# Moving feature tile 0 of a normed input to another byte distance from the weight tiles, in a two-layer decoder trunk

## The chip, the cores and the metric

One core of a Trainium2 chip runs the whole program in one launch. The metric is the device time of one execution in microseconds (us). TensorE (PE, with its weight loads as PEld) multiplies, VectorE (DVE) and ScalarE (ACT) split operands and do the elementwise work, SyncE (SP) issues nearly all weight transfers.

## The reference, cut to what matters

Two layers on 256 tokens of width 1024; everything is float32.

```python
x = x + short_conv_mixer(rms_norm(x, a_norm), a_w_in, a_conv, a_w_out)      # mixer A
x = x + conv_glu_ffn(rms_norm(x, f_norm[0]), f_w_up[0], f_conv[0], ...)     # first feed-forward
k, v = shared_kv(rms_norm(x, kv_norm), w_k, w_v)
x = x + moba_attention(rms_norm(x, b_norm), b_w_q, b_w_o, k, v, ...)        # mixer B
x = x + conv_glu_ffn(rms_norm(x, f_norm[1]), f_w_up[1], f_conv[1], ...)     # second feed-forward
return rms_norm(x, final_norm)

def conv_glu_ffn(h, w_up, conv_w, conv_b, w_down):
    u = causal_dwconv(h @ w_up, conv_w) + conv_b
    g, v = split(u, 2)                        # d_ff = 2816 each
    return (silu(g) * v) @ w_down
```

## The kernel before, in words

**Products.** The float32 product of a weight tile and an input tile is taken as three products of fp32r parts: high weight by high input, high weight by low input, low weight by high input. `mm3` (L164 to L166) issues these three matmuls. In each, the 128x128 weight part is the stationary operand, loaded by PEld, and a 128x256 input part (128 features, 256 tokens) is the moving one. The normed input is held as `xh` and `xl`, eight feature tiles (k = 0 to 7) of 256 columns, 1024 bytes per partition each. The norm's gain is in them; its row factor is applied to the result, so a unit can start before the norm's sum is known.

**Units.** A weight unit is one column block: "B" units of 128x2048 (two output tiles, `m` = 2) and "S" units of 128x1024. SP loads `raw`, ACT writes the high part `hi` (L86), DVE the low part `lo` (L92). `up_step` runs the 48 matmuls of a B unit (8 feature tiles, 2 output tiles, 3 products) or the 24 of an S unit into one PSUM bank. A feed-forward has 22 up units, and 22 down units that follow with a lag of three. In the first feed-forward the down products are `mm3` too (24 matmuls of 256 columns, gated hidden parts `sh`, `sl` moving). In the second they are `token_bank` (L189 to L191): 12 matmuls of 512 columns, with the hidden parts stationary and the weights moving. The V projection (L555 to L558) also has its weights moving and its input parts stationary.

**Order.** The order of each engine is that of the code (a manual schedule). PE runs through the stream of units almost without a pause. What stands between units, and is called a break below, is `rstd_cols` (L305: 128x1 matmuls of the sum of squares), `rstd_rows` (L319: a matmul that spreads the row factor), `bias_table` (L330), and in mixer B the transposes, scores and probability products. `rstd_cols` and `rstd_rows` come once in each of mixer A (within units MC[1] and MC[2]), the first feed-forward (unit 1 and behind it), the V projection and the second feed-forward (unit 1 and behind it). `bias_table` stands in mixer A ahead of unit MC[4].

**Addresses.** `shifted` (L242) makes the tiles of `xh` and `xl`: 64 floats longer than needed, with the data from float 48, that is 192 bytes in. The hidden parts `sh` and `sl` begin at float 16 of tiles that the pool places 128 bytes further, modulo 256, than the weight tiles. Every `hi` and `lo` tile and both buffers of `xh` and `xl` are placed at one remainder modulo 256 bytes, and every step within them is a multiple of 256 bytes. So whenever an input part moves against a weight part, the moving operand starts 192 bytes behind the stationary one, modulo 256. This is called the distance below. Where a weight moves against an input part (the V projection, the second feed-forward's down products) it is 64.

Of the kernel before, what the change touches and what calls it, by code (L numbers as in the profile page):

```python
# [12 lines left out]
F32R = mybir.dt.float32r  # L13
I32 = mybir.dt.int32
AF = mybir.ActivationFunctionType
OP = mybir.AluOpType

S = 256
D = 1024
KT = D // 128  # L20
# [12 lines left out]
P_AN, P_KVN, P_BN, P_FN, P_FIN, P_CONV, P_FCW, P_FCB = 0, 8, 16, 24, 40, 48, 72, 336  # L33
# [4 lines left out]
def f32(ap):  # L38
    return ap.bitcast(F32)
# [3 lines left out]
def yoco_kernel(ctx: ExitStack, tc: tile.TileContext, t: dict, out: bass.AP):  # L43
    nc = tc.nc
    V, A, G, PE = nc.vector, nc.scalar, nc.gpsimd, nc.tensor
# [3 lines left out]
    act = ctx.enter_context(tc.tile_pool(name="act", bufs=2))  # L49
# [12 lines left out]
    class Unit:  # L62


        def __init__(self, src, n, slots=(0, 1, 2)):
            self.src, self.n, self.tag = src, n, "B" if n == BIG else "S"
            self.raw = self.hi = self.lo = None
            self.used = False
            mine = by_tag[self.tag]
            self.at = len(mine)  # L70
            last = {s: max([u.at for u in mine if u.slot == s], default=-1) for s in slots}
            self.slot = min(slots, key=lambda s: (last[s], s))
            self.prev = mine[last[self.slot]] if last[self.slot] >= 0 else None
            mine.append(self)
# [22 lines left out]
    def hi(tag, part=0, parts=1):  # L97

        n = ptr[tag][0]
        if n < len(by_tag[tag]) and (by_tag[tag][n].prev is None or by_tag[tag][n].prev.used):  # L100
            by_tag[tag][n].split_hi(part, parts)
            ptr[tag][0] += part == parts - 1
# [11 lines left out]
    MC = [Unit(t["w_mc"][j], BIG) for j in range(KT)]  # L114
# [48 lines left out]
    def mm3(o, wh, wl, xh, xl, start, stop):  # L163
        PE.matmul(o, wh, xh, start=start, stop=False, skip_group_check=True)  # L164
        PE.matmul(o, wh, xl, start=False, stop=False, skip_group_check=True)  # L165
        PE.matmul(o, wl, xh, start=False, stop=stop, skip_group_check=True)  # L166

    def up_step(u, o, xh, xl, m, ks=range(KT)):

        assert u.lo is not None  # L170
        wh, wl = u.v(u.hi, m), u.v(u.lo, m)
        for k in ks:
            for i in range(m):
                mm3(o[:, i, :], wh[:, k, i, :], wl[:, k, i, :], xh[:, k, :], xl[:, k, :],
                    start=(k == 0 and i == 0), stop=(k == KT - 1))
        u.used = ks[-1] == KT - 1

    def down_bank(u, b, acc, hh, hl, first, last):
# [61 lines left out]
    def shifted(pool, name, tag, rows, **kw):  # L240

        t = pool.tile([128, rows * S + 64], F32R, name=name, tag=tag, **kw)  # L242
        return t[:, 48:48 + rows * S].rearrange("p (k s) -> p k s", s=S)

    def parts_tiles():
        return shifted(act, "xh", "xh", KT), shifted(act, "xl", "xl", KT)

    def scaled_hi(x, gain, ks, xh, order=same):
        for k in ks:
# [10 lines left out]
    def sum_squares(sq, half, order=same):  # L260

        f = 4 * half
        V.tensor_add(sq[:, f:f + 2, :], sq[:, f:f + 2, :], sq[:, f + 2:f + 4, :])
        if half:
            V.tensor_add(sq[:, 0:2, :], sq[:, 0:2, :], sq[:, 4:6, :])
            V.tensor_add(sq[:, 2, :], order(sq[:, 0, :]), order(sq[:, 1, :]))
# [1 line left out]
    def square_tile():  # L268
        return act.tile([128, KT, S], F32, name="sq", tag="oh", bufs=1)

    def boundary(acc, x, gain, order=same):

        xh, xl = parts_tiles()
        sq = square_tile()
        for q in range(5):
            if q < 4:
                V.tensor_add(x[:, 2 * q:2 * q + 2, :], acc[q], x[:, 2 * q:2 * q + 2, :])
                scaled_hi(x, gain, (2 * q, 2 * q + 1), xh, order)
            if q:
                scaled_lo(x, gain, (2 * q - 2, 2 * q - 1), xh, xl, order)  # L280
                squares(x, sq, q - 1)
        sum_squares(sq, 0)
        for part in range(2):
            lo("B", part, 2)
        sum_squares(sq, 1, order)
        return xh, xl, sq
# [77 lines left out]
    for q in range(4):  # L364
# [3 lines left out]
        if q == 2:  # L368
            sum_squares(sq, 0)
    sum_squares(sq, 1)  # L370
    hi("S")
    lo("S")
    rr = None
# [24 lines left out]
        zl()  # L398

    mc[1] = acc_bank()  # L400
    up_step(MC[1], mc[1], xh, xl, 2, range(0, 6))
    _, dg = rstd_cols(sq)
    for q in range(4):
        hi("B", q, 4)
        lo("B", q, 4)
    hi("S")
    hi("B")
    up_step(MC[1], mc[1], xh, xl, 2, range(6, 8))
    mb[1] = acc_bank()
    up_step(MB[1], mb[1], xh, xl, 1)  # L410
    mc[2] = up_bank()
    up_step(MC[2], mc[2], xh, xl, 2, range(0, 2))
    rr = rstd_rows(dg)
    A.activation(rr[:, 1, :], rr[:, 0, :], AF.Square)
    lo("S")
    up_step(MC[2], mc[2], xh, xl, 2, range(2, 8))
    mb[2] = psum.tile([128, 512], F32, name="misc", bufs=1).rearrange("p (a s) -> p a s", s=S)
    up_step(MB[2], mb[2], xh, xl, 1)
    for i in range(2):
# [17 lines left out]
    bias_table()  # L437
    for j in range(4, KT):
        mc[j] = up_bank()
        up_step(MC[j], mc[j], xh, xl, 2)  # L440
        o = mixer_a(j, "S")
        mb[j] = up_bank()
        up_step(MB[j], mb[j], xh, xl, 1)
        hi("S")
        mixer_b(j, o, "B" if j < KT - 1 else "S")
        if j < KT - 1:
            lo("S")
        if j == KT - 3:
            lo("B")
        down_step(MO[j - 2], acc, z[j - 2])  # L450
        hi("S")
        if j == KT - 1:
            lo("S")
    down_last(MO[KT - 2:], acc, [z[KT - 2], z[KT - 1]])
    xh, xl, sq = boundary(acc, xT, P_FN)
    hi("S")


# [2 lines left out]
    def ffn(layer, xh, xl, sq, bank=down_bank, between=None):  # L461
        ub, hd, low = {}, {}, {}
        up, dn = UP[layer], DN[layer]

        def conv(j, last=False):
            c0 = 2 * FJ * layer + j
            cw = [[par(P_FCW, 3 * (c0 + half * FJ) + n) for n in range(3)] for half in range(2)]
            u = tmp.tile([128, 2, S], F32, name="u", bufs=2)
            V.tensor_mul(u, ub[j], rr[:, 0:1, :].to_broadcast([128, 2, S]))  # L469
            if j:  # L470
                low[j - 1]()
            if not last:
                lo("B")
            o = tmp.tile([128, 2, S], F32, name="cv", bufs=2)
            for half in range(2):
                A.activation(o[:, half, :], u[:, half, :], AF.Identity, scale=cw[half][2],  # L476
                             bias=par(P_FCB, c0 + half * FJ))
            hi("B")
            for back in (1, 2):
                for half in range(2):  # L480
                    tap(o[:, half, :], u[:, half, :], cw[half][2 - back], back)
            return o

        def gate(j, o, last=False):
            sl = tmp.tile([128, S], F32, name="sl", tag="sc", bufs=3)
            hi("S")
            A.activation(sl, o[:, 0, :], AF.Silu)
            lo("S", 0, 1 + last)
            hid = tmp.tile([128, S], F32, name="hid", tag="pr", bufs=4)
            V.tensor_mul(hid, sl, o[:, 1, :])  # L490
            hd[j], zh, low[j] = split_act(hid, S)
            zh()
            if last:
                lo("S", 1, 2)
                low[j]()

        acc = None
        for i in range(FJ):
            ub[i] = up_bank()
            if i == 1:  # L500
                up_step(up[1], ub[1], xh, xl, 2, range(0, 3))
                _, dg = rstd_cols(sq)
                lo("S")
                A.activation(first, ones[:, 0:1], AF.Silu)
                up_step(up[1], ub[1], xh, xl, 2, range(3, 8))
                rr = rstd_rows(dg)
                gate(0, conv(0))
            else:
                up_step(up[i], ub[i], xh, xl, 2)
            last = i == FJ - 1  # L510
            if i:
                o = conv(i, last)
                if not last:
                    gate(i, o)
            if i == 0 and between:
                between()
            if i >= LAG:
                if i == LAG:
                    acc = [acc_bank() for _ in range(4)]
                down_step(dn[i - LAG], acc, hd[i - LAG], first=(i == LAG), bank=bank)  # L520
            if last:
                gate(i, o, True)
            elif i == FJ - 2:
                hi("S")
                lo("S")
            if i == 0:
                hi("B")
        if bank is token_bank:
            token_last(dn[FJ - 3:], acc, [hd[j] for j in range(FJ - 3, FJ)])
        else:  # L530
            down_step(dn[FJ - 3], acc, hd[FJ - 3])
            down_last(dn[FJ - 2:], acc, [hd[FJ - 2], hd[FJ - 1]])
        return acc
# [223 lines left out]
    wo(4)  # L757
    wo(5)
    down_last(WO[KT - 2:], acc, [(oh[:, j, :], ol[:, j, :]) for j in (KT - 2, KT - 1)])
    xh, xl, sq = boundary(acc, xT, P_FN + KT)  # L760
    hi("B")
    lo("B")
    hi("S")
# [128 lines left out]
```

## Time and profile before

| | |
|---|---|
| runs of the kernel | 590.6, 594.22, 589.56 us (median 590.6) |
| the profiled execution | 590.07 us |
| its span | 588.2 us |
| outside the span | 1.87 us |
| mean granted TensorE clock over the span | 0.996 |
| PE busy | 579.7 us, 99% of the span, 4745 matmuls |
| PEld busy | 564.4 us, 96% |
| DVE busy, ACT busy | 460.6 us (78%), 359.0 us (61%) |

The span is from the first instruction to the end of the last; PE's busy time counts matmuls that overlap in a pipeline, so that the pace of the stream is read from the starts of the matmuls and not from the busy share.

### The profile page before, as it was taken

To read this page: it belongs to the slowest core of one execution; us is meant where nothing else is said; L and a number is where in the kernel's file an instruction comes from. 1 tells how busy PE (TensorE), PEld (TensorE's weight loads), DVE (VectorE), ACT (ScalarE), POOL (GpSimd) and SP (SyncE) were. 2 spreads that over 40 slices of the span, in tenths; PEclk is the share of its full clock that TensorE was granted. 3 is DMA by queue.
4 is the path that set the end of the run, shared out by engine and by line. 5 is a ranking of instruction groups with operands and counts; after the bars stand their busy time and mean duration, and the time that the engine had idled before them with its cause. 6 is when DMAs were issued, how large, how long until landed. Compare 5 with 4: busy or idle time off the path is not lost.

```text
span 588.2 us, 11533 instructions
## 1 busy us (share of the span) xinstructions
PE 579.7 (99%) x4745; PEld 564.4 (96%) x4745; DVE 460.6 (78%) x779; ACT 359.0 (61%) x568; POOL 3.7 (1%) x15
## 2 busy tenths in 40 slices
PE   9999999999999999999999999999999999999995
PEld 8999999999999999999999999999999999999994
DVE  5898769888887778877987997668997778777865
ACT  7665337566665556555758998648675455545443
POOL 0000000000000000000000000000000000000001
PEclk9999999999999999999999999999999999999998
DMA  8985583447545654555456564424555654553111
GB/s 292 402 283 188 167 299 109 155 144 266 183 167 198 216 215 178 168 194 180 144 170 236 184 217 162 152 100 150 209 198 196 216 191 160 188 214 119 61 37 72
DMA packets 24236, 108.51 MB, mean 184 GB/s; under 512 B 2759, under 2 KB 5496, under 8 KB 16248
## 3 DMA queue, kind: packets, MB, share of 16 engines
q1 hardware_dynamic: 23864, 107.46, 51.5%
q8 instruction: 37, 0.61, 0.4%
q10 hardware_dynamic: 320, 0.32, 0.2%
q14 instruction: 15, 0.12, 0.1%
HBM read 106.70 MB, written 1.07 MB: 183 GB/s over the span
## 4 chain that ended last, share of the span: by engine, by line
PE 96%; DMA 1%; ACT 1%; SPq 0%; DVE 0%; issue 0%; POOLq 0%; POOL 0%; DVEq 0%; ACTq 0%
PE up L164 20%; PE up L166 20%; PE up L165 20%; PE acc L164 6%; PE acc L165 6%; PE acc L166 6%; PE acc L189 3%; PE acc L190 3%; PE acc L191 3%; PE acc L599 1%; PE acc L555 1%; PE acc L557 1%; PE acc L558 1%; DMA xres<-xT 1%; PE up L558 0%; PE up L555 0%
## 5 line engine op out<-in xcount | busy, mean ns | idle before, releaser
L164 PE MATMUL up<-xh,hiB 128*128 128x256 f32 x944 | 264.7, 280 | 0.0
L166 PE MATMUL up<-xh,loB 128*128 128x256 f32 x944 | 263.5, 279 | 0.2 <-DVE loB L92 0.2
L165 PE MATMUL up<-xl,hiB 128*128 128x256 f32 x944 | 263.1, 279 | 0.0
L164 PEld LDWEIGHTS up<-xh,hiB 128*128 128x128 f32 x944 | 177.8, 188 | 1.8 <-issue 0.6
L166 PEld LDWEIGHTS up<-xh,loB 128*128 128x128 f32 x944 | 178.9, 189 | 0.7 <-DVE loB L92 0.6
L165 PEld LDWEIGHTS up<-xl,hiB 128*128 128x128 f32 x944 | 177.5, 188 | 0.8
L92 DVE TENSOR_TENSOR loB<-rawB,hiB 128x2048 fp32r<-128x2048 f32 (+2 forms) x75 | 147.6, 1973 | 3.2 <-ACT hiB L86 3.0
L86 ACT ACTIVATE hiB<-rawB 128x2048 fp32r<-128x2048 f32 (+1 forms) x73 | 123.6, 1696 | 18.9 <-issue 6.3
L476 ACT ACTIVATE cv<-u,pk 128x256 f32<-128x256 f32 x88 | 48.2, 595 | 76.4 <-DVE u L469 76.4
L92 DVE TENSOR_TENSOR loS<-rawS,hiS 128x1024 fp32r<-128x1024 f32 (+2 forms) x73 | 83.7, 1147 | 14.0 <-ACT hiS L86 13.7
L348 DVE SCALAR_TENSOR_TENSOR cv<-u,pk,cv 128x255 f32<-128x255 f32 x192 | 81.4, 479 | 2.6 <-ACT cv L476 1.7
L469 DVE TENSOR_TENSOR u<-up,rr 128x512 f32<-128x512 f32 x44 | 30.4, 690 | 62.2 <-PE up L166 60.9
L86 ACT ACTIVATE hiS<-rawS 128x1024 fp32r<-128x1024 f32 (+1 forms) x71 | 71.6, 1010 | 11.4 <-PE acc L165 7.1
L166 PE MATMUL acc<-sh,loS 128*128 128x256 f32 x240 | 66.6, 277 | 0.0
L164 PE MATMUL acc<-sh,hiS 128*128 128x256 f32 x240 | 66.6, 277 | 0.0
L165 PE MATMUL acc<-sl,hiS 128*128 128x256 f32 x240 | 66.6, 277 | 0.0
L345 ACT ACTIVATE sh<-hid 128x256 fp32r<-128x256 f32 x52 | 21.7, 417 | 59.7 <-DVE hid L490 54.9
L164 PEld LDWEIGHTS acc<-sh,hiS 128*128 128x128 f32 x240 | 45.3, 189 | 0.0
L166 PEld LDWEIGHTS acc<-sh,loS 128*128 128x128 f32 x240 | 45.1, 188 | 0.0
L165 PEld LDWEIGHTS acc<-sl,hiS 128*128 128x128 f32 x240 | 45.0, 188 | 0.0
L189 PE MATMUL acc<-hiS,sh 128*128 128x512 f32 (+1 forms) x89 | 34.9, 393 | 0.0
L190 PE MATMUL acc<-loS,sh 128*128 128x512 f32 (+1 forms) x89 | 34.8, 391 | 0.0
(155 smaller groups left out, 756.6 us busy)
## 6 DMA issues: line engine op xcount, KB each, us to landing
rawB<-w_up SPq DMA_DIRECT2D x44, 1024.0 KB, 4.8
rawS<-w_dn SPq DMA_DIRECT2D x44, 512.0 KB, 3.4
rawB<-w_qk SPq DMA_DIRECT2D x8, 1024.0 KB, 4.9
rawB<-w_mc SPq DMA_DIRECT2D x6, 1024.0 KB, 8.7
rawS<-w_mo SPq DMA_DIRECT2D x8, 512.0 KB, 5.0
rawB<-w_v SPq DMA_DIRECT2D x4, 1024.0 KB, 4.7
rawS<-w_o SPq DMA_DIRECT2D x8, 512.0 KB, 3.9
rawS<-w_mb SPq DMA_DIRECT2D x7, 512.0 KB, 5.7
```

Source lines behind the costliest of these rows:

```text
L86: A.activation(self.hi[:, c], self.raw[:, c], AF.Copy)
L92: V.tensor_sub(self.lo[:, c], self.raw[:, c], f32(self.hi[:, c]))
L164: PE.matmul(o, wh, xh, start=start, stop=False, skip_group_check=True)
L165: PE.matmul(o, wh, xl, start=False, stop=False, skip_group_check=True)
L166: PE.matmul(o, wl, xh, start=False, stop=stop, skip_group_check=True)
L189: PE.matmul(o, hh[:, tok], u.hi[:, f], start=first, stop=False, skip_group_check=True)
L190: PE.matmul(o, hh[:, tok], u.lo[:, f], start=False, stop=False, skip_group_check=True)
L191: PE.matmul(o, hl[:, tok], u.hi[:, f], start=False, stop=last, skip_group_check=True)
L345: return (h, lw), lambda: A.activation(h, src, AF.Copy), lambda: V.tensor_sub(lw, src, f32(h))
L348: V.scalar_tensor_tensor(o[:, back:], u[:, :S - back], w, o[:, back:], op0=OP.mult, op1=OP.add)
L469: V.tensor_mul(u, ub[j], rr[:, 0:1, :].to_broadcast([128, 2, S]))
L476: A.activation(o[:, half, :], u[:, half, :], AF.Identity, scale=cw[half][2], bias=par(P_FCB, c0 + half * FJ))
```

## The change

Tile 0 gets a second place in a longer tile. `Rows` replaces `shifted` for `xh` and `xl`: nine feature rows and 64 floats. Its first row, `again`, starts at float 32, 128 bytes in; the eight rows of before start at float 48 of the next row, so that their distance stays 192. With `moved=True`, which only the second feed-forward's input has, feature tile 0 itself is written to and read from `again`, in all 22 units. Elsewhere `tile_0_again` copies tile 0 there (ACT the high part, DVE the low part), and `up_step(..., again=True)` reads the copy for k = 0: in the parts of MC[1] and MC[2] that stand behind the two breaks of mixer A, in MC[4], in the part of unit 1 behind `rstd_cols` and in unit 2 of the first feed-forward. There the parts ahead of a break take tiles 1 to 6 (MC[1]), 1 and 2 (MC[2]) or 1 to 3 (unit 1) in place of 0 to 5, 0 and 1, or 0 to 2, and tile 0 comes first behind the break. The distance of all other matmuls modulo 256 stays as it was. The longer tiles take 4 KB more of each partition.

```diff
-    def up_step(u, o, xh, xl, m, ks=range(KT)):
+    def up_step(u, o, xh, xl, m, ks=range(KT), first=0, again=False):
         for k in ks:
+            h, lw = (xh.again, xl.again) if again and k == 0 else (xh[:, k, :], xl[:, k, :])
             for i in range(m):
-                mm3(o[:, i, :], wh[:, k, i, :], wl[:, k, i, :], xh[:, k, :], xl[:, k, :],
-                    start=(k == 0 and i == 0), stop=(k == KT - 1))
+                mm3(o[:, i, :], wh[:, k, i, :], wl[:, k, i, :], h, lw,
+                    start=(k == first and i == 0), stop=(k == KT - 1))
...
-    def parts_tiles():
-        return shifted(act, "xh", "xh", KT), shifted(act, "xl", "xl", KT)
+    class Rows:
+        def __init__(self, name, moved):
+            t = act.tile([128, (KT + 1) * S + 64], F32R, name=name, tag=name)
+            self.again = t[:, 32:32 + S]
+            self.rows = t[:, 48 + S:48 + S + KT * S].rearrange("p (k s) -> p k s", s=S)
+            self.moved = moved
+        def __getitem__(self, i):
+            return self.again[:, i[2]] if self.moved and i[1] == 0 else self.rows[i]
+    def parts_tiles(moved=False):
+        return Rows("xh", moved), Rows("xl", moved)
+    def tile_0_again(xh, xl):
+        A.activation(xh.again, f32(xh[:, 0, :]), AF.Copy)
+        V.tensor_copy(xl.again, f32(xl[:, 0, :]))
...
     sum_squares(sq, 1)
+    tile_0_again(xh, xl)
     hi("S")
...
-    up_step(MC[1], mc[1], xh, xl, 2, range(0, 6))
+    up_step(MC[1], mc[1], xh, xl, 2, range(1, 7), first=1)
     _, dg = rstd_cols(sq)
...
-    up_step(MC[1], mc[1], xh, xl, 2, range(6, 8))
+    up_step(MC[1], mc[1], xh, xl, 2, (0, 7), first=1, again=True)
...
-    up_step(MC[2], mc[2], xh, xl, 2, range(0, 2))
+    up_step(MC[2], mc[2], xh, xl, 2, (1, 2), first=1)
     rr = rstd_rows(dg)
...
-    up_step(MC[2], mc[2], xh, xl, 2, range(2, 8))
+    up_step(MC[2], mc[2], xh, xl, 2, (0, 3, 4, 5, 6, 7), first=1, again=True)
...
-        up_step(MC[j], mc[j], xh, xl, 2)
+        up_step(MC[j], mc[j], xh, xl, 2, again=(j == 4))
...
     xh, xl, sq = boundary(acc, xT, P_FN)
+    tile_0_again(xh, xl)
...
-                up_step(up[1], ub[1], xh, xl, 2, range(0, 3))
+                up_step(up[1], ub[1], xh, xl, 2, range(1, 4), first=1)
                 _, dg = rstd_cols(sq)
...
-                up_step(up[1], ub[1], xh, xl, 2, range(3, 8))
+                up_step(up[1], ub[1], xh, xl, 2, (0, 4, 5, 6, 7), first=1, again=True)
...
-                up_step(up[i], ub[i], xh, xl, 2)
+                up_step(up[i], ub[i], xh, xl, 2, again=(i == 2))
...
-    xh, xl, sq = boundary(acc, xT, P_FN + KT)
+    xh, xl, sq = boundary(acc, xT, P_FN + KT, moved=True)
```

On PE the list of matmuls keeps its length, its names and the places of the breaks; only which feature tile stands where, and the address of tile 0, differ. DVE and ACT get two instructions each. On DVE in mixer A, before (`sq` is the sum of squares, `lo` the low weight part of an S unit, `nw` the chain for the row factor):

```order
L266 TENSOR_TENSOR sq<-sq 128x256
L92 TENSOR_TENSOR loS_267<-rawS,hiS_265 128x1024
L309 TENSOR_SCALAR nw<-misc 128x2
L290 TENSOR_SCALAR nw<-nw 128x2
L292 TENSOR_TENSOR nw<-nw 128x2
```

and of the changed kernel, at the same place:

```order
L284 TENSOR_TENSOR sq<-sq 128x256
L264 CAST xl<-xl 128x256
L92 TENSOR_TENSOR loS_269<-rawS,hiS_267 128x1024
L327 TENSOR_SCALAR nw<-misc 128x2
L308 TENSOR_SCALAR nw<-nw 128x2
L310 TENSOR_TENSOR nw<-nw 128x2
```

The copy of the low part stands behind the sum of squares and ahead of one weight split and the row factor's chain. On ACT at the start of the first feed-forward, before (`hiS` is the next weight unit's high part, `rr` the row factor):

```order
L250 ACTIVATE xh<-xres,pk 128x256 x2
L258 ACTIVATE sq<-xres 128x512 x2
L86 ACTIVATE hiS_1307<-rawS 128x1024
L86 ACTIVATE hiB_1358<-rawB 128x2048
L504 ACT_TABLE_LOAD
```

and of the changed kernel:

```order
L268 ACTIVATE xh<-xres,pk 128x256 x2
L276 ACTIVATE sq<-xres 128x512 x2
L263 ACTIVATE xh<-xh 128x256
L86 ACTIVATE hiS_1311<-rawS 128x1024
L86 ACTIVATE hiB_1362<-rawB 128x2048
L524 ACT_TABLE_LOAD
```

The copy of the high part stands behind the squares and ahead of two weight splits. The other DVE and ACT copies stand in the same way at the other place.

## Rows read from the trace of the kernel before

**Rows 1.** The page: busy time by engine, and the chain that ended last.
```profile
PE 579.7 (99%) x4745; PEld 564.4 (96%) x4745; DVE 460.6 (78%) x779; ACT 359.0 (61%) x568; POOL 3.7 (1%) x15
...
PE 96%; DMA 1%; ACT 1%; SPq 0%; DVE 0%; issue 0%; POOLq 0%; POOL 0%; DVEq 0%; ACTq 0%
```
**Rows 2.** Stretches: length, busy us (count) of PE, PEld, DVE, ACT, POOL; granted clock.
```profile
60.00:100.00 40.00, 40.00 (x342) 40.00 (x342) 28.77 (x41) 18.03 (x25) 0.00 (x0) 1.00 0.63 211
120.00:160.00 40.00, 40.00 (x356) 40.00 (x355) 35.10 (x56) 26.26 (x35) 0.00 (x0) 1.00 0.50 178
19.82:106.58 86.76, 86.76 (x730) 85.94 (x730) 70.88 (x114) 47.48 (x61) 0.00 (x0) 1.00 0.65 226
107.15:287.70 180.55, 180.55 (x1592) 180.50 (x1592) 146.07 (x228) 108.04 (x152) 0.00 (x0) 1.00 0.51 184
288.27:297.00 8.73, 8.73 (x74) 8.68 (x74) 8.35 (x23) 3.19 (x5) 0.00 (x0) 1.00 0.50 169
403.12:572.58 169.46, 169.46 (x1220) 159.68 (x1220) 131.71 (x204) 94.60 (x128) 0.00 (x0) 1.00 0.46 168
```
**Rows 3.** PE in time, first feed-forward: an up unit's start, the down unit behind it.
```profile
116.34 0.28 PE L164 MATMUL up<-xh,hiB 128*128 128x256 f32 x1
...
121.78 0.28 PE L164 MATMUL acc<-sh,hiS 128*128 128x256 f32 x1
```
**Rows 4.** PE in time, second feed-forward: a down unit, the up unit behind it.
```profile
418.27 0.40 PE L189 MATMUL acc<-hiS,sh 128*128 128x512 f32 x1
...
419.21 0.39 PE L190 MATMUL acc<-loS,sh 128*128 128x512 f32 x1
...
421.04 0.28 PE L164 MATMUL up<-xh,hiB 128*128 128x256 f32 x1
...
426.69 0.40 PE L189 MATMUL acc<-hiS,sh 128*128 128x512 f32 x1
```
**Rows 5.** PE in time, behind the first break of the first feed-forward.
```profile
106.59 0.50 PE L305 MATMUL misc<-ones,sq 128*128 128x1 f32 x4
...
107.27 0.28 PE L166 MATMUL up<-xh,loB 128*128 128x256 f32 x1
...
108.63 0.28 PE L166 MATMUL up<-xh,loB 128*128 128x256 f32 x1
```
**Rows 6.** PE in time, behind the first break of the second feed-forward.
```profile
402.56 0.50 PE L305 MATMUL misc<-ones,sq 128*128 128x1 f32 x4
...
403.24 0.28 PE L166 MATMUL up<-xh,loB 128*128 128x256 f32 x1
...
404.65 0.28 PE L166 MATMUL up<-xh,loB 128*128 128x256 f32 x1
```
**Rows 7.** PE in time, from the V projection to the first Q/K unit.
```profile
296.95 0.28 PE L558 MATMUL acc<-hiB,xl 128*128 128x256 f32 x1
297.06 0.29 PE L164 MATMUL up<-xh,hiB 128*128 128x256 f32 x1
297.19 0.28 PE L165 MATMUL up<-xl,hiB 128*128 128x256 f32 x1
297.31 0.28 PE L166 MATMUL up<-xh,loB 128*128 128x256 f32 x1
...
298.67 0.28 PE L166 MATMUL up<-xh,loB 128*128 128x256 f32 x1
```
**Rows 8.** DVE in time, mixer A and first feed-forward; in brackets the idle time before.
```profile
18.42 0.43 DVE L266 TENSOR_TENSOR sq<-sq 128x256 f32<-128x256 f32 x1
...
22.52 2.50 DVE L92 TENSOR_TENSOR loB<-rawB,hiB 128x512 fp32r<-128x512 f32 x4
...
107.12 0.16 DVE L309 TENSOR_SCALAR nw<-misc 128x2 f32<-128x2 f32 x1 [1.18 <-PE misc L305]
```
**Rows 9.** ACT in time, the same two places.
```profile
19.43 2.19 ACT L86 ACTIVATE hiB<-rawB 128x512 fp32r<-128x512 f32 x4 [1.78 <-DMA rawB<-w_mc]
...
104.55 1.92 ACT L86 ACTIVATE hiB<-rawB 128x2048 fp32r<-128x2048 f32 x1 [1.91 <-PE up L165]
```

More of the change, by code (lines that the diff above doesn't have):

```diff
@@ L269, in square_tile, with boundary @@
         return act.tile([128, KT, S], F32, name="sq", tag="oh", bufs=1)
-    def boundary(acc, x, gain, order=same):
-        xh, xl = parts_tiles()
+    def boundary(acc, x, gain, order=same, moved=False):
+        xh, xl = parts_tiles(moved)
         sq = square_tile()
```

## The prediction

> **What bounds the kernel now.** I read the page first: PE is busy for 579.7 of 588.2 us and 96% of the chain that ended last is PE, so waits of the other engines cost nothing unless they reach it [rows 1]. A stream without pauses can be shortened only by its pace, so next I read the stretches and, in time order, the distances between starts of matmuls. The reader is to see that the same kind of matmul (128x128 weights, 256 columns) runs at two paces. In 40 us of the first feed-forward 356 are counted, in 40 us of mixer A 342, both at a granted clock of 1.00, the 2.4 GHz level, so the clock is not the difference [rows 2]. An up unit's 48 matmuls take 121.78 - 116.34 = 5.44 us in the first feed-forward, 113.3 ns each, and 426.69 - 421.04 = 5.65 us in the second, 117.7 ns each [rows 3, 4]. I call these the 113 and the 118 pace; one matmul differs by 4.4 ns, one unit by 0.21 us.
>
> Where does a pace begin? Behind a break. Both feed-forwards come into `rstd_cols` in the same way. From 107.27 to 108.63, 12 matmuls take 1.36 us (113 pace) [rows 5]; from 403.24 to 404.65, 12 take 1.41 (118 pace) [rows 6]. The code, the shapes and the distance of 192 bytes are the same, so the pace is not set by the distance alone: the stream seems to fall into one of two rhythms, and keeps it, since every later matmul stands in the same relation to its weight load. The first feed-forward keeps the 113 pace over 180.55 us (1592 matmuls, 113.4 ns each), the second the 118 pace over 169.46, mixer A over 86.76 us with 730 [rows 2].
>
> Is there a place where the 118 pace ends without a break? One. The V projection (8.73 us for 74, with one break in them [rows 2]) runs at distance 64, the Q/K units behind it at 192. Over that seam the starts are 0.11, 0.13 and 0.12 us apart, and the next 12 matmuls take 298.67 - 297.31 = 1.36 us: the 113 pace [rows 7]. A change of distance can end the long rhythm. It need not: the second feed-forward goes from 192 to 64 and back at every down unit, and each up unit still has 5.65 us [rows 4].
>
> **The change part by part.** It gives six matmuls another distance, 128, directly behind each of five breaks, and in each of 22 units of the second feed-forward. It adds or removes no matmul. Its worth is how much of the 118 pace it ends.
>
> Mixer A, with the first feed-forward's start: from 19.82 to 106.58 there are 730 matmuls [rows 2], of which about 10 belong to breaks. 720 x 4.4 ns = 3.2 us, if tile 0 behind the first break brings the 113 pace and the copies behind the next two restore it.
>
> Second feed-forward: 1220 matmuls in 169.46 us [rows 2], among them 19 down units of 12; the other 990 or so have 256 columns. 990 x 4.4 ns = 4.4 us. The down units' 512-column matmuls are seen at no other rhythm. In the one shown the first four take 419.21 - 418.27 = 0.94 us, the next eight 421.04 - 419.21 = 1.83, 0.229 each [rows 4]; four at that pace would take 0.915, so entering from the 118 pace costs about 0.025 us, 0.5 us for 19. The bounds for these 228 are nothing, and twice a 256-column matmul's gain, 228 x 8.8 ns = 2.0 us; a loss of the same kind is not excluded, if 64 behind 128 has a longer rhythm of its own. I take 0.5, the value nearest to a row.
>
> The new distance itself: 22 units change it twice. The seam in rows 7 cost 0.02 us at most beyond the 113 pace on its first matmul; a seam within a rhythm shows less than the 0.01 us that the rows resolve. Bounds: 0 and 44 x 0.02 = 0.9 us. I take 0.1. Whether six matmuls at 128 run at 113, at 118 or at a third pace no row shows. If each lost another 4.4 ns beyond the 118 pace, 162 of them would cost 0.7 us; if they ran free of either rhythm's loss the gain would be of the same size. I take zero.
>
> The two copies on DVE and two on ACT: near 0.43 us each, by the 128x256 row of `sq` [rows 8]. ACT has idle times of 1.78 and 1.91 us behind the copies' places, DVE 1.18 at the second [rows 8, 9]. In mixer A DVE has no such gap, and the row factor's chain and the split of `loB` for MC[2] come 0.43 us later. Its four quarters begin at 22.52 and take 2.50 us in all [rows 8]; MC[2] now wants its second quarter with its second tile. That quarter is done near 23.8, or 24.2 with the copy; PE begins MC[2] near 23.9 and wants it 0.7 us later, near 24.6, less the 0.2 us that it has gained by then. So it is covered by about 0.2 us; without the cover the price is at most 0.4. MC[1] wants its last quarter about 1 us sooner, and this is split well before. SP's queue issues the same transfers in the same order.
>
> The sum, against the profiled execution's own 590.07 us (span 588.2 and 1.87 outside it): -3.2 - 4.4 - 0.5 + 0.1 = -8.0, so 582.1, said as 582. The median of the runs shown is 590.6, 0.5 above the profiled one; the highest is 594.22, and since the rhythm is drawn at breaks, such a spread could be one more stretch at the 118 pace (an estimate: no trace of that run is here).
>
> **The rivals.** *Half of it.* The tile works in one of the two stretches: mixer A alone gives 590.1 - 3.2 = 586.9, the second feed-forward alone 590.1 - 4.8 = 585.3. For it: there the tile returns with every unit, so one chance in 22 is enough to begin, while mixer A has three copies in all; and the second feed-forward's down units, at 64, may bring back the long rhythm each time. Against it: both stretches have the same three products and distances.
>
> *It does not do what it says.* The rhythm comes from the moment at which PE comes out of a break, the distance is without effect: 590, give or take what the breaks redraw. For it: rows 5 and 6, two paces at one distance, and the second feed-forward's seams, which end nothing. Against it: rows 7. The Trainium skill speaks for this rival: "TensorE: Matmul & The Clock Gate", Part 2, says that the moving operand and the weight load have independent SBUF read ports, so that loading the next weights takes nothing from the running matmul. By that rule the distance could not matter at all, and the time would stay 590. The rule also leaves no reason for two paces at one clock, which this trace has.
>
> *Slower.* The first feed-forward has the 113 pace by a draw. The change reorders its unit 1 and puts 128 behind both its breaks. If the seam from 128 back to 192 ends in the 118 pace there, nothing ends that again until the V projection, because all of it stands at 192: 1592 x 4.4 ns = 7.0 us [rows 2], 597.1 if nothing is gained elsewhere, 592 to 594 if one of the other stretches improves. It decides from the point where its first seam leaves the pace; against it stands that no seam from the 113 pace into the 118 pace is seen in the rows.
>
> **How the numbers follow.** Forecast 0.46; half of it 0.26; no effect 0.15; slower 0.13. The low end is the full gain with the down units' upper bound: 590.1 - 3.2 - 4.4 - 2.0 = 580.5, less 0.3 for the V projection's 74 matmuls and 0.7 for six free matmuls per unit: 579.5. The high end has to take in no effect and part of the slower case: 592. About 0.13 is left out. Some 1% (5.9 us) is what a measurement of this kernel can tell from no change. Faster by over 1% needs the forecast, or the second feed-forward with its down units at the upper bound: 0.47. Within 1%: the rest of half, no effect, and slower offset by a gain: 0.42. Slower by over 1%: the first feed-forward lost with nothing gained: 0.11.
>
> **What would show it.** Right: up units of 5.44 us in the second feed-forward, some 340 to 355 matmuls per 40 us in mixer A nearer to 355, the record length of matmuls equal in all three stretches, the first feed-forward unchanged. Half: one stretch alone. No effect: 5.65 us units again in spite of the moved tile. Wrong in sign: units of 5.65 us in the first feed-forward. PE idle near 24 us would show the copy's delay uncovered. A pace of the six tile-0 matmuls other than the neighbours' would show a price of the distance itself.

## The result, and the profile after

The changed kernel takes 594.41 us (median of 22 runs, 593.39 to 595.29), the kernel before 590.22 (22 runs, 589.56 to 594.56): the ratio is 1.0053 [1.0037, 1.0069], slower by about 4 us, where a gain was forecast, and outside the predicted range of 579.5 to 592. The runs of the kernel before lie in two groups, 16 near 590.1 and 6 near 594.3 us, which is why the interval is wide; all 22 of the changed kernel lie in one. The profiled executions took 594.58 and 590.07 us, with spans of 592.5 and 588.2.

The page of the changed kernel shows the same bound as [rows 1], PE throughout:

```profile
PE 583.1 (98%) x4745; PEld 568.1 (96%) x4745; DVE 461.0 (78%) x781; ACT 359.7 (61%) x570; POOL 3.6 (1%) x15
...
PE 97%; DMA 1%; ACT 1%; DVE 0%; issue 0%; SPq 0%; POOLq 0%; POOL 0%; DVEq 0%; ACTq 0%
```

The same stretches as in [rows 2], of the changed kernel (length, busy us and count of PE, PEld, DVE, ACT, POOL; granted clock):

```profile
60.00:100.00 40.00, 40.00 (x342) 40.00 (x341) 28.75 (x41) 18.03 (x25) 0.00 (x0) 1.00 0.61 211
120.00:160.00 40.00, 40.00 (x342) 40.00 (x341) 33.46 (x53) 24.91 (x34) 0.00 (x0) 1.00 0.47 172
107.17:294.70 187.53, 187.53 (x1592) 187.48 (x1592) 146.30 (x228) 108.04 (x152) 0.00 (x0) 1.00 0.49 178
411.05:576.90 165.85, 165.85 (x1218) 156.51 (x1218) 131.41 (x203) 94.31 (x128) 0.00 (x0) 1.00 0.47 171
```

In 40 us of the first feed-forward 342 matmuls are counted where 356 were: its 1592 matmuls now take 187.53 us instead of 180.55. Mixer A has its 342 as before, the second feed-forward is shorter by 3.6 us for two matmuls less. The clock is 1.00 throughout.

PE in time, of the changed kernel: behind the first break of mixer A, at its second, at the second break of the first feed-forward and its units, then the second feed-forward. The lines are now L323 for `rstd_cols`, L337 for `rstd_rows`, L190 for `token_bank`.

```profile
19.46 0.50 PE L323 MATMUL misc<-ones,sq 128*128 128x1 f32 x4
...
20.84 0.28 PE L166 MATMUL acc<-xh,loB 128*128 128x256 f32 x1
...
25.26 0.28 PE L166 MATMUL up<-xh,loB 128*128 128x256 f32 x1
25.38 0.59 PE L337 MATMUL misc<-dg,ones 128*128 128x256 f32 x2
...
26.05 0.28 PE L166 MATMUL up<-xh,loB 128*128 128x256 f32 x1
...
27.23 0.28 PE L164 MATMUL up<-xh,hiB 128*128 128x256 f32 x1
...
108.49 0.28 PE L164 MATMUL up<-xh,hiB 128*128 128x256 f32 x1
...
110.19 0.28 PE L164 MATMUL up<-xh,hiB 128*128 128x256 f32 x1
...
110.53 0.59 PE L337 MATMUL misc<-dg,ones 128*128 128x256 f32 x2
...
116.63 0.28 PE L164 MATMUL up<-xh,hiB 128*128 128x256 f32 x1
...
122.28 0.28 PE L164 MATMUL acc<-sh,hiS 128*128 128x256 f32 x1
...
420.16 0.28 PE L164 MATMUL up<-xh,hiB 128*128 128x256 f32 x1
...
425.82 0.40 PE L190 MATMUL acc<-hiS,sh 128*128 128x512 f32 x1
...
428.62 0.28 PE L164 MATMUL up<-xh,hiB 128*128 128x256 f32 x1
...
429.80 0.28 PE L165 MATMUL up<-xl,hiB 128*128 128x256 f32 x1
...
434.12 0.39 PE L190 MATMUL acc<-hiS,sh 128*128 128x512 f32 x1
...
436.86 0.28 PE L164 MATMUL up<-xh,hiB 128*128 128x256 f32 x1
```

Behind `rstd_cols` with tile 0 at 128 the 113 pace begins: 39 matmuls from 20.84 to 25.26 take 4.42 us. Behind `rstd_rows` with tile 0 at 128 it is gone: 10 matmuls from 26.05 take 1.18. The same happens in the first feed-forward: 15 in 1.70 us from 108.49, the 113 pace, then `rstd_rows` at 110.53, and a unit of 122.28 - 116.63 = 5.65 us where it was 5.44 [rows 3]. Unit 3 of the second feed-forward, the second behind its `rstd_rows`, still takes 5.66. The next comes out of the 512-column down products: its first 10 matmuls take 1.18, the 118 pace, the other 38 run at 113.7, in all 5.50 us, against 5.65 before [rows 4]; the down unit behind it takes 2.74, against 2.77.

By sections, in the profiled executions. Each runs from one `rstd_cols` to the next, so that the first feed-forward's row holds the 72 matmuls of the V projection that stand ahead of its `rstd_cols`, and the last row ends some 0.6 us behind the last matmul of PE:

| us | before | after | difference | predicted |
|---|---|---|---|---|
| up to mixer A's `rstd_cols` | 19.25 | 19.46 | +0.2 | 0 |
| mixer A | 87.34 | 87.16 | -0.2 | -3.2 |
| first feed-forward | 181.11 | 188.09 | +7.0 | 0 |
| V projection and attention | 114.86 | 115.48 | +0.6 | 0 |
| second feed-forward | 179.29 | 176.05 | -3.2 | -4.8 |

The differences add up to +4.4; the spans differ by 4.3. The first feed-forward alone turns the sign.

### The profile page after: what moved, and what is told of

Its sections match the earlier page's. It is cut to its first block, busy times and chain, and to the rows that moved or that the text cites. A ratio compares the mean times of both kernels' runs of the same rounds, so it can differ in the third digit from the quotient of the medians.

```text
span 592.5 us, 11536 instructions
## 1 busy us (share of the span) xinstructions
PE 583.1 (98%) x4745; PEld 568.1 (96%) x4745; DVE 461.0 (78%) x781; ACT 359.7 (61%) x570; POOL 3.6 (1%) x15
## 4 chain that ended last, share of the span: by engine, by line
PE 97%; DMA 1%; ACT 1%; DVE 0%; issue 0%; SPq 0%; POOLq 0%; POOL 0%; DVEq 0%; ACTq 0%
PE up L164 20%; PE up L165 20%; PE up L166 20%; PE acc L164 7%; PE acc L165 7%; PE acc L166 7%; PE acc L192 3%; PE acc L191 3%; PE acc L190 3%; PE acc L619 1%; PE acc L575 1%; PE acc L578 1%; PE acc L577 1%; DMA xres<-xT 1%; PE up L578 0%; PE up L575 0%
## 5 line engine op out<-in xcount | busy, mean ns | idle before, releaser
L192 PE MATMUL acc<-hiS,sl 128*128 128x512 f32 (+1 forms) x89 | 34.9, 392 | 0.0
```

Source lines behind the costliest of these rows:

```text
L192: PE.matmul(o, hl[:, tok], u.hi[:, f], start=False, stop=last, skip_group_check=True)
```

## The experiments

**The stretch that lost.** The theory from the profile after: the copies behind `rstd_rows` destroy the 113 pace that those behind `rstd_cols` bring. Its rivals: the second feed-forward's units cost something, or the copies and the new order of tiles do, whatever the distance. The first run takes one copy away, that of unit 2 in the first feed-forward:

```diff
-                up_step(up[i], ub[i], xh, xl, 2, again=(i == 2))
+                up_step(up[i], ub[i], xh, xl, 2)
```

> The changed kernel, but unit 2 of the first feed-forward reads tile 0 at its old distance of 192 bytes; nothing else differs. Theory (the copy at distance 128 directly behind rstd_rows throws the first feed-forward from the 113 into the 118 pace): that stretch goes back to units of 5.44 us and the time falls by about 1592 x 4.4 ns = 7 us, from 594.4 to 587.4. Rival (the pace is drawn anew by any shift in time, the copy has no part in it): units of 5.65 us stay, 594.4.

Measured: 586.87 us (586.18 to 587.45), 0.9912 [0.988, 0.9943] of the kernel before. Its stretches (columns as above):

```profile
60.00:100.00 40.00, 40.00 (x342) 40.00 (x341) 28.77 (x43) 18.40 (x26) 0.00 (x0) 1.00 0.60 209
120.00:160.00 40.00, 40.00 (x355) 40.00 (x355) 35.10 (x57) 26.26 (x35) 0.00 (x0) 1.00 0.53 184
```

Six matmuls back at 192, and 7.5 us come back: the first feed-forward counts 355 again, mixer A stays at 342.

**The second feed-forward alone.** Before, with `Rows` and `moved=True` for the second feed-forward and nothing else of the change:

```diff
-    xh, xl, sq = boundary(acc, xT, P_FN + KT)
+    xh, xl, sq = boundary(acc, xT, P_FN + KT, moved=True)
```

> The kernel before, with tile 0 at distance 128 in all units of the second feed-forward and nothing else of the change. Theory (distance 128 shortens those units where they stand behind a down unit, and the first feed-forward is lost only through its own copies): first feed-forward at 5.44 us a unit, second near 5.50, 590.2 - 3.2 = 587.0. Rival (the second feed-forward's gain comes from the order of tiles at its breaks or from the draw): its units stay at 5.65, 590.2.

Measured: 586.56 us (586.29 to 587.2), 0.991 [0.9882, 0.9939]. PE in time, behind the two breaks of its second feed-forward:

```profile
402.67 0.50 PE L318 MATMUL misc<-ones,sq 128*128 128x1 f32 x4
...
403.23 0.28 PE L165 MATMUL up<-xl,hiB 128*128 128x256 f32 x1
...
406.53 0.28 PE L166 MATMUL up<-xh,loB 128*128 128x256 f32 x1
406.65 0.60 PE L332 MATMUL misc<-dg,ones 128*128 128x256 f32 x2
...
407.20 0.29 PE L165 MATMUL up<-xl,hiB 128*128 128x256 f32 x1
...
408.16 0.28 PE L164 MATMUL up<-xh,hiB 128*128 128x256 f32 x1
408.27 0.28 PE L165 MATMUL up<-xl,hiB 128*128 128x256 f32 x1
...
409.40 0.28 PE L166 MATMUL up<-xh,loB 128*128 128x256 f32 x1
```

Here tiles 3 to 7 stand behind `rstd_cols`, at 192: 28 matmuls from 403.23 to 406.53 take 3.30 us, the 118 pace. Behind `rstd_rows` comes tile 0 at 128: 8 in 0.96 us, then 10 from 408.27 in 1.13. The same break and the same address that ended the 113 pace in the changed kernel end the 118 pace here. So 128 behind `rstd_rows` does not bring a pace; it exchanges one for the other.

**The copies without the distance.** The changed kernel with `again` at the distance of the other tiles, so that copies, order and instructions stay:

```diff
-            self.again = t[:, 32:32 + S]
+            self.again = t[:, 48:48 + S]
```

> The changed kernel with the second place of tile 0 at float 48 instead of 32: the same copies, order of tiles and longer tiles, but every distance 192. Theory (the distance does it): first feed-forward at 5.44, second at 5.65 us a unit, mixer A at the 118 pace, about 590.3, like before. Rival (the copies, the order and the shift in time do it): the second feed-forward keeps its 5.50 and the first its 5.65, about 594.4.

Measured: 590.72 us (590.25 to 594.79, four of ten runs near 594.3), 1.0022 [0.9992, 1.0052]. Its stretches:

```profile
60.00:100.00 40.00, 40.00 (x342) 40.00 (x341) 28.76 (x42) 18.03 (x25) 0.00 (x0) 1.00 0.60 211
120.00:160.00 40.00, 40.00 (x356) 40.00 (x355) 35.10 (x56) 26.25 (x35) 0.00 (x0) 1.00 0.50 178
```

All as before. The copies and the order cost nothing that the times show; the address of `again` makes the whole difference to the changed kernel. All weight tiles lie at one remainder modulo 256, so neither this run nor a later one tells the distance from the moving operand's own address.

**Copies behind one kind of break only.** First only behind `rstd_cols` (MC[2], MC[4] and unit 2 at 192), called the `rstd_cols` version below:

```diff
-    up_step(MC[2], mc[2], xh, xl, 2, (0, 3, 4, 5, 6, 7), first=1, again=True)
+    up_step(MC[2], mc[2], xh, xl, 2, (0, 3, 4, 5, 6, 7), first=1)
...
-        up_step(MC[j], mc[j], xh, xl, 2, again=(j == 4))
+        up_step(MC[j], mc[j], xh, xl, 2)
...
-                up_step(up[i], ub[i], xh, xl, 2, again=(i == 2))
+                up_step(up[i], ub[i], xh, xl, 2)
```

> The changed kernel with the copy used only behind rstd_cols (MC[1], unit 1 of the first feed-forward); MC[2], MC[4] and unit 2 of the first feed-forward read tile 0 at 192. Theory (behind rstd_cols distance 128 brings the 113 pace, behind rstd_rows it loses it, and rstd_rows followed by 192 keeps the pace it had): mixer A at the 113 pace from 21 us at least to bias_table at 47, first feed-forward at 5.44 a unit: 594.4 - 7.0 - 0.8 = 586.6, or 584 if the pace survives bias_table too. Rival (draw by time shift): no pattern, anything from 587 to 594.4, and mixer A at 118 behind rstd_rows.

Measured: 583.84 us (583.65 to 584.5), 0.987 [0.9825, 0.9916]. Its stretches:

```profile
60.00:100.00 40.00, 40.00 (x355) 40.00 (x354) 30.63 (x46) 20.43 (x29) 0.00 (x0) 1.00 0.60 209
120.00:160.00 40.00, 40.00 (x355) 40.00 (x354) 33.37 (x52) 26.01 (x35) 0.00 (x0) 1.00 0.55 201
```

Mixer A has 355 for the first time. The 113 pace lasts through `rstd_rows` and through `bias_table`, all at 192, to the end of the first feed-forward. This version beats both kernels.

Then only behind `rstd_rows`, to part two theories: A, that a break changes the pace in a fixed way that depends on the pace before it; B, that 128 behind `rstd_cols` is good and 128 behind `rstd_rows` bad as such.

```diff
-    up_step(MC[1], mc[1], xh, xl, 2, (0, 7), first=1, again=True)
+    up_step(MC[1], mc[1], xh, xl, 2, (0, 7), first=1)
...
-        up_step(MC[j], mc[j], xh, xl, 2, again=(j == 4))
+        up_step(MC[j], mc[j], xh, xl, 2)
...
-                up_step(up[1], ub[1], xh, xl, 2, (0, 4, 5, 6, 7), first=1, again=True)
+                up_step(up[1], ub[1], xh, xl, 2, (0, 4, 5, 6, 7), first=1)
```

> The changed kernel with the copy used only behind rstd_rows (MC[2], unit 2 of the first feed-forward); MC[1], MC[4] and unit 1 of the first feed-forward read tile 0 at 192. Theory A (each kind of break with each distance maps the pace before onto the pace behind: rstd_cols then 192 exchanges 113 and 118, rstd_cols then 128 gives 113, rstd_rows then 192 keeps the pace, rstd_rows then 128 exchanges the two, bias_table keeps it): mixer A 118 from 20 to 25 us, then 113 to its end; first feed-forward 118 for its unit 1, then 5.44 us a unit: close to 584. Theory B (128 behind rstd_rows always brings the 118 pace): mixer A and first feed-forward at 118, 594.

Measured: 584.44 us (584.16 to 585.13), 0.9904 [0.989, 0.9919]: theory A. PE in time behind its `rstd_rows` of mixer A:

```profile
25.80 0.60 PE L337 MATMUL misc<-dg,ones 128*128 128x256 f32 x2
...
26.35 0.29 PE L165 MATMUL up<-xl,hiB 128*128 128x256 f32 x1
...
27.31 0.28 PE L164 MATMUL up<-xh,hiB 128*128 128x256 f32 x1
27.42 0.28 PE L165 MATMUL up<-xl,hiB 128*128 128x256 f32 x1
...
28.89 0.28 PE L166 MATMUL up<-xh,loB 128*128 128x256 f32 x1
```

The stream comes into this break at the 118 pace, runs 8 matmuls in 0.96 us and then 13 from 27.42 in 1.47, 113 each. The same edit as in the changed kernel, the opposite effect.

The third takes unit 1's copy out of the `rstd_cols` version as well (that version's edits, and the last one above), so that the first feed-forward comes into `rstd_cols` at 113 and has 192 behind it:

> As the run with the copy behind rstd_cols alone, but with unit 1 of the first feed-forward at 192 too, so that MC[1] alone uses a copy. Theory A (rstd_cols then 192 exchanges the paces): mixer A at 113, so the first feed-forward comes out of its rstd_cols at 118 and keeps 5.65 us a unit: 583.8 + 7.0 = 590.8, with no line of the first feed-forward's own changed but the order of tiles in one unit. Theory B (each break has a pace of its own, as in the kernel before, where this break gave 113): 5.44 us a unit, 583.8.

Measured: 591.09 us (590.65 to 591.57), 0.9999 [0.9977, 1.0022]: theory A again. Its stretches:

```profile
60.00:100.00 40.00, 40.00 (x355) 40.00 (x354) 30.70 (x45) 20.53 (x29) 0.00 (x0) 1.00 0.57 208
120.00:160.00 40.00, 40.00 (x342) 40.00 (x341) 32.95 (x51) 25.95 (x35) 0.00 (x0) 1.00 0.51 186
```

Mixer A keeps the 113 pace, and by that the first feed-forward, which comes in at 118 in the kernel before and leaves at 113, comes in at 113 and leaves at 118. A gain of 3.2 us upstream is paid for with 7 downstream.

**All tiles at 128.** The kernel before with all eight tiles from float 32:

```diff
-        return t[:, 48:48 + rows * S].rearrange("p (k s) -> p k s", s=S)
+        n = 32 if tag in ("xh", "xl") else 48
+        return t[:, n:n + rows * S].rearrange("p (k s) -> p k s", s=S)
```

> The kernel before with all eight feature tiles of every normed input at distance 128 (the data from float 32 of their tiles); hidden parts stay at 192. It measures the steady pace at 128 by itself. Theory A (the six matmuls at 128 run at 118 to 120 in every trace so far, so 128 has no 113 pace of its own and is of use only as a seam): up units of 5.65 us or more in all stretches, 600 us or more. Rival (128 is the better distance and the price is paid only at the seams to 192): up units of 5.44 us or less, 585 or below.

Measured: 600.72 us, one run. PE in time, an up unit of its first feed-forward:

```profile
117.05 0.28 PE L164 MATMUL up<-xh,hiB 128*128 128x256 f32 x1
...
122.75 0.28 PE L164 MATMUL acc<-sh,hiS 128*128 128x256 f32 x1
...
123.47 0.28 PE L164 MATMUL acc<-sh,hiS 128*128 128x256 f32 x1
...
125.51 0.28 PE L164 MATMUL up<-xh,hiB 128*128 128x256 f32 x1
```

5.70 us for 48, 118.8 each; the second feed-forward's units take 5.76, 120 each. No quick pace at 128 is seen in this run. The down unit behind, whose hidden parts stay at 192, follows without a break: its last 18 matmuls, from 123.47 to 125.51, take 2.04 us, the 113 pace. So a seam from 48 matmuls at 128 to 192 does bring 113, without a break, and the next unit at 128 ends it again.

**A seam in every unit of the first feed-forward**, in place of its copies: `moved=True` there too.

```diff
-    xh, xl, sq = boundary(acc, xT, P_FN)
-    tile_0_again(xh, xl)
+    xh, xl, sq = boundary(acc, xT, P_FN, moved=True)
```

> The changed kernel with tile 0 of the first feed-forward at 128 in all its units, as in the second, and without the copies there. Theory A (unit 2 behind rstd_rows goes from 113 to 118; a seam 192, 128, 192 within the 118 pace does not end it, only one behind the second feed-forward's 512-column matmuls at distance 64 does): units of 5.65 us to the end of the first feed-forward, 594 to 595. Rival (every unit's tile 0 is a new chance): 113 pace after a few units, 587.5 to 588.

Measured: 594.9 us, one run. Its stretch:

```profile
120.00:160.00 40.00, 40.00 (x342) 40.00 (x341) 33.43 (x52) 24.56 (x33) 0.00 (x0) 1.00 0.49 176
```

Some 20 seams end nothing there: without a break, six matmuls at 128 between others at 192 leave the 118 pace as it is.

The trace of this run shows one thing more. The stream comes into mixer A's `rstd_cols` at the 118 pace, 83 matmuls in 9.78 us, though up to there its code is that of the changed kernel, which comes in at 113 (86 in 9.76 from 9.58 to 19.34):

```profile
9.86 0.28 PE L164 MATMUL up<-xh,hiB 128*128 128x256 f32 x1
...
19.64 0.28 PE L166 MATMUL acc<-xh,loB 128*128 128x256 f32 x1
```

All other traces with the first unit at 192 come in at 113. So the pace that the program starts with can differ from run to run; here the copy behind `rstd_cols` still brings 113.

**The rest of the second feed-forward.** The `rstd_cols` version with 192 directly behind the second feed-forward's `rstd_rows`, by giving unit 2 tile 1 first:

```diff
-                up_step(up[i], ub[i], xh, xl, 2)
+                up_step(up[i], ub[i], xh, xl, 2, *(((1, 0, 2, 3, 4, 5, 6, 7), 1) if layer and i == 2 else ()))
```

> The kernel with the copy behind rstd_cols alone, and in unit 2 of the second feed-forward tile 1 (at 192) stands directly behind rstd_rows, with tile 0 (at 128) second. Theory A (rstd_rows then 192 keeps the 113 pace of unit 1; a seam 192, 128, 192 does not end a pace): units 2 and 3 go from 118 to 113, 0.4 us less, 583.4. Rival (a seam to 128 without a break exchanges the paces too): units 2 and 3 stay at 118 up to the first down unit, 583.8.

Measured: 583.44 us (583.16 to 583.93), 0.988 [0.9835, 0.9925]. PE in time, its unit 3:

```profile
409.45 0.29 PE L164 MATMUL up<-xh,hiB 128*128 128x256 f32 x1
...
414.93 0.39 PE L190 MATMUL acc<-hiS,sh 128*128 128x512 f32 x1
```

5.48 us, against 5.66 for unit 3 of the changed kernel. It has the lowest median of the case. Its runs overlap those of the `rstd_cols` version (583.65 to 584.5), so the 0.4 us are not told by the times; the unit shows 0.2 of them.

**The second group of times.** Two more runs of the kernel before and one of the copies without the distance, unchanged, for a trace of a run near 594.3:

> The kernel before once more, for a look at its second group of times: 6 of the first 22 runs of it, and 4 of 10 of the run with all distances at 192, lay near 594.3 and the others near 590.1, while no kernel with tile 0 of the second feed-forward at 128 had such a group. Theory (the 4.2 us lie in the second feed-forward, where a second long rhythm can be drawn): if the time is near 594, its cycles of up and down unit are longer than 8.42 us and the stretches before it are as they were. Rival (one of the other stretches is drawn differently): mixer A or the first feed-forward differs. If the time is near 590 it tells nothing.

> The same kernel and the same expectations as the run before it; a second chance of seeing the group near 594.

> The changed kernel with all distances at 192 once more: 4 of its 10 runs lay near 594.3. Same two expectations as for the kernel before: a time near 594 with cycles longer than 8.42 us in the second feed-forward, or with a longer mixer A or first feed-forward; near 590 it tells nothing.

Measured: 589.65, 590.07 and 589.82 us. None fell in that group, so where its 4.2 us lie was not seen. Over all its runs, the kernel before has 17 of 65 near 594.3.

The theory above, a long rhythm in the second feed-forward, was not tested by these runs. A rival follows from the run just named with 118 at its start. If the kernel before comes into mixer A's `rstd_cols` at 118, the break, with 192 behind it, gives 113 by the rule seen so far; the first feed-forward then comes in at 113 and leaves its `rstd_cols` at 118. An estimate from traces: mixer A 84.18 in place of 87.34 us and the first feed-forward 188.14 in place of 181.11 (both from the run at 591.09), and 83 matmuls x 4.4 ns = 0.4 at the start, so 590.1 - 3.2 + 7.0 + 0.4 = 594.3. The 47 runs of the five kernels that were run more than once with 128 behind that break, which brings 113 from either pace, have one group. Against it stand the second feed-forward alone and the `rstd_rows` copies only, with 192 there and no such run in 12; at 17 in 65 that happens by chance in 3 of 100 cases. No trace decides.

## Why the prediction was wrong

*The bound and the two paces* held: the kernels differ by the stretches that run at one pace or the other, at a granted clock of 1.00 in all rows shown.

*Mixer A, -3.2 predicted, -0.2 measured.* The step that failed is "if tile 0 behind the first break brings the 113 pace and the copies behind the next two restore it". Its first half is right (4.42 us for 39 matmuls from 20.84). The copy behind the second break ended the pace instead, and that of MC[4] behind `bias_table` left the 118 pace as it was. What is left is 40 matmuls x 4.4 ns = 0.2 us. The same 3.2 us are there to be had with these two copies away, as the `rstd_cols` version shows (mixer A in 84.18 us).

*Second feed-forward, -4.8 predicted, -3.2 measured.* The mechanism was right, the term was too large in two ways. Units 2 and 3 stay at 118, behind `rstd_rows` with tile 0 at 128, and every later unit takes 5.50 us and not 5.44, since the stream needs tile 0's six matmuls and a few more to come to the 113 pace. I took zero for the new distance's own matmuls; they run at the 118 pace (10 in 1.18 us from 428.62). The down units gave 0.03 each, as taken. 18 pairs of units at 0.18 make 3.2.

*First feed-forward, nothing predicted, +7.0 measured.* This is the rival "slower", with its price right (1592 x 4.4 ns = 7.0) and its place nearly so: a seam behind a break, but the second one's, at `rstd_rows`, where the rival let the first seam decide. Its chance of 0.13 was too low, for a reason that can be named: I read [rows 5, 6], one break with two outcomes, as a draw, and wrote that both feed-forwards come into `rstd_cols` in the same way. They do not. These rows of the kernel before stand ahead of the two breaks:

```profile
105.05 0.28 PE L166 MATMUL up<-xh,loB 128*128 128x256 f32 x1
...
106.47 0.28 PE L166 MATMUL up<-xh,loB 128*128 128x256 f32 x1
...
401.08 0.28 PE L166 MATMUL up<-xh,loB 128*128 128x256 f32 x1
...
402.44 0.28 PE L166 MATMUL up<-xh,loB 128*128 128x256 f32 x1
```

The 12 matmuls from 105.05 take 1.42 us, the 118 pace, those from 401.08 take 1.36, the 113 pace, and each stretch comes out at the other. These rows I had not read. With "no seam from the 113 pace into the 118 pace is seen" I had looked only at seams without a break.

*The rest.* The copies were hidden as predicted: 0.29 us on DVE in mixer A, and no gap on PE near 24 us. V and attention lost 0.6, mostly in Q/K units that the seam of [rows 7] no longer brings to 113.

*"It does not do what it says"* is refuted by the changed kernel and the copies without the distance, whose instructions differ in an address alone: 342 and 356 matmuls in 40 us of the first feed-forward, at 1.00 of the clock. Their times, 594.41 and 590.72 us, would not do by themselves, since four of the ten runs without the distance lie near 594.3. Clear of that are 594.41 against 586.87, two kernels that differ in the address of six matmuls, and 600.72 with all tiles at 128. The Trainium skill ("TensorE: Matmul & The Clock Gate", Part 2) says that the moving operand and the weight load read SBUF through independent ports; by that the distance could not matter. The measurement decides against that consequence. Whether the ports, or something behind them, make the difference no run here shows.

What the runs show in place of the draw at each break, each line from the traces of the kernels named:

| break, distance directly behind it (the rest at 192) | pace behind it | seen in |
|---|---|---|
| `rstd_cols`, 192 | the other one | before and second feed-forward alone: 118, 113, 118 in turn; `rstd_rows` copies only; the run at 591.09 |
| `rstd_cols`, 128 | 113, from either | the changed kernel, three places; `rstd_cols` copies only; first feed-forward moved |
| `rstd_rows`, 192 | the same | before, three places; `rstd_cols` copies only |
| `rstd_rows`, 128 | the other one | the changed kernel, three places (113 to 118); second feed-forward alone and `rstd_rows` copies only (118 to 113) |
| `bias_table`, 128 or 192 | the same | the changed kernel (128, at 118); before (192, at 118); `rstd_cols` copies only (192, at 113) |
| none, six matmuls at 128 | the same | first feed-forward moved (118); unit 3 of the run at 583.44 (113) |
| none, 48 matmuls at 128, then 192 | 113 | all tiles at 128, its first feed-forward's down units |
| none, 512-column down units, then 128 | 113 | the changed kernel, every later unit |

The table is a record of these programs, not a mechanism: why a break with one address exchanges the paces was not found. The pace alone does not settle everything either. The run at 591.09 us and the changed kernel both come into the V projection at 118 and stay there; behind it the Q/K units run at 113 in the first and at 118 in the second.

## What to carry to other kernels

When one stream bounds a kernel and runs at two paces, read the pace ahead of each break as well as behind it before calling it chance: two rows more would have shown that this break was no draw. A break that exchanges paces makes gains interact, so that a gain upstream is paid for downstream; edits to such places are tried one at a time, and the whole stretch behind each is counted, not the place itself. Where copies or order come with an address, run them once with the old address: here that one run parted the two.

## What the runs showed that was not expected

Six matmuls that read their input at distance 128 in place of 192 move the whole kernel by 7.5 us (594.41 against 586.87). Over all versions with the same matmuls the time runs from 583.44 to 600.72 us, at one clock. The 113 pace holds over 237 us and 2000 matmuls (from 47.36 to 284.50 us in the kernel at 583.44), through down units and breaks. And one program can have two groups of times 4.2 us apart: in the kernel before (6 of the 22 runs beside the changed kernel) and in the copies without the distance (4 of 10), but in none of 59 runs of the seven kernels that have tile 0 of the second feed-forward at 128 and were run more than once. Five of the seven also have 128 behind mixer A's `rstd_cols`, so these counts do not tell which of the two places it is. No trace of such a run was caught, so its cause stays open.
